# The opening of a hybrid encoder block by halves of the tokens, in another written order, with unread products of a constant on TensorE between its first transposes

## The chip, the core and the metric

The kernel runs on one core of a Trainium2 chip. The time is the device time of one execution in microseconds; lower is better. The engines of a core work side by side from queues of their own: TensorE (PE: matrix products and transposes, with PEld its weight loads), VectorE (DVE), ScalarE (ACT), GpSimd (POOL), and SyncE (SP), which here only issues DMA transfers. Each engine takes its instructions in the order in which they are written, and waits on semaphores for the others.

## The reference, cut to what matters

One layer of an encoder over 512 tokens of width 1024: a SwiGLU feed-forward half step, a token mixer, a second feed-forward half step, each behind an adaptive normalisation. The change lies in the first normalisation and the first columns of the first feed-forward product.

```python
sc = jax.nn.silu(c)
mod = sc @ w_ada[l] + b_ada[l]                 # 1024 -> 9 * 1024
sh1, s1, g1, sh2, s2, g2, sh3, s3, g3 = jnp.split(mod, N_MOD, axis=-1)
h = _modulate(x, sh1, s1)                      # RMSNorm(x) * (1 + s1) + sh1
x = x + 0.5 * g1[:, None, :] * _swiglu(h, ffn1_w_in[l], ffn1_w_out[l])
...                                            # mixer, second feed-forward
```

## The kernel before

Activations lie transposed: a tile has 128 of the 1024 features in its partitions and the tokens along its columns. So the 512 tokens, which come as four blocks of 128 rows in two halves of 512 features (eight tiles `xt`), are first turned on TensorE (`raw`, four transposes and one copy by VectorE for each tile). Products keep nearly full precision: activation and weight are each split into a high and a low part (`hh`/`hl`, `wh`/`wl`), and a product is three passes, high by high, low by high, high by low (lines 304 to 306 elsewhere, 412, 428 and 429 for the first feature tile).

`phase0` is the opening. For each of the eight feature tiles kt it loads 1 MB of `w_ada` (tile `ar`, two transfers) and 384 KB of `ffn1_w_in` (tile `wr`), forms shift and scale of these 128 features (`phase0_cols`, 16 narrow passes on TensorE; `columns`, two products that turn the result into columns, and two small steps on VectorE: `sh`, `s`), normalises the tile (`modulate`: `hm` on VectorE, `hh` on ScalarE, `hl` on VectorE), splits the weights (`wh` cast by ScalarE, `wl` by VectorE), and adds 18 passes of 512 columns to six accumulators `pu`. These are the first six of the 44 columns of tiles of the feed-forward's first product; the others follow in `units`.

Before that stand the sums of squares of x (ScalarE, eight times line 358, each with a read of the accumulator), the mean and its power of -1/2 on GpSimd (`rms_cols`, line 188: `ry`), and for the first feature tile a way of its own: the tokens are scaled by `r` while still untransposed (`xn`), turned (line 394), and modulated (lines 396 to 401). For the other tiles r is spread over the partitions by a product of ones with a diagonal matrix (`dg`, line 476), copied to `rb` (line 414).

The opening is written out in one order, and every instruction of it is made to follow the one before on its engine (`in_order`), so nothing in it is moved by a scheduler. SP issues the transfers in the order of the calls; there are three buffers for `ar` and four each for `wr`, `wh`, `wl`, and five PSUM buffers `pb` beside three `pa`.

Of the kernel before, what the change touches and what calls it, by code (L numbers as in the profile page):

```python
# [19 lines left out]
P = 128  # L20
# [68 lines left out]
class Block:  # L89
# [226 lines left out]
    def setup(self):  # L316
        nc, ins = self.nc, self.ins
        self.vecs = self.slot(s="vecs")[:, :P]
        self.load(self.vecs[72:80, :], ins["c"].rearrange("o (t p) -> (o t) p", p=P))
        self.load(self.vecs[0:72, :], ins["b_ada"].rearrange("o (t p) -> (o t) p", p=P))  # L320
        xd = ins["x"][0]
        self.xtok = [[self.slot(s="xt") for _ in range(2)] for _ in range(NB)]
        for b in range(NB):
            for j in range(2):
                self.load(self.xtok[b][j], xd[b * P:(b + 1) * P, j * NT:(j + 1) * NT])
# [7 lines left out]

    def phase0(self):

        nc = self.nc
# [3 lines left out]
        loads = [self.phase0_load(0), self.phase0_load(1)]  # L340
        pv = self.aux()
        nc.tensor.transpose(pv[:, :80], self.vecs[:80, :], self.ident[:80, :80])
        self.sc = self.const([P, 8], s="sc")
        nc.scalar.activation(self.sc, pv[:, 72:80], AF.Silu)
        self.vT = self.const([P, 72], s="vT")
        nc.vector.tensor_copy(self.vT, pv[:, :72])
        self.sel4 = self.const([P, 1], s="sel4")
        nc.vector.tensor_reduce(out=self.sel4, in_=self.ident[:, 0:P:32], axis=AX.X, op=ALU.add)

        def raw(b, j):  # L350
# [3 lines left out]
            nc.vector.tensor_copy(xall[:, 4 * j:4 * j + 4, b * P:(b + 1) * P], pt.rearrange("p (t c) -> p t c", t=4))  # L354

        tiles = [(b, j) for b in range(NB) for j in range(2)]
        for b, j in tiles:
            nc.scalar.activation(self.slot(s="jk"), self.xtok[b][j], AF.Square, accum_out=ss[:, 2 * b + j:2 * b + j + 1])
        for i in (2, 0, 1, 3):
            raw(*tiles[i])  # L360
        v = self.small(NB, "v")
        nc.vector.tensor_reduce(out=v, in_=ss.rearrange("p (b j) -> p b j", j=2), axis=AX.X, op=ALU.add)
        r = self.rms_cols(v, NB, D)
        for i in (4, 5, 6):
            raw(*tiles[i])
        self.c1, self.c2 = self.const([P, KT], s="sh"), self.const([P, KT], s="s1")
        self.new_h()

        def columns(kt, sg, pg):
            k = slice(kt, kt + 1)  # L370
            for m in range(2):
                nc.tensor.matmul(pg[:, 256 + m:257 + m], sg[:, m * P:m * P + P], self.sel4, start=True, stop=True)
            nc.vector.tensor_tensor(out=self.c1[:, k], in0=pg[:, 256:257], in1=self.vT[:, k], op=ALU.add)
            nc.vector.scalar_tensor_tensor(out=self.c2[:, k], in0=pg[:, 257:258], scalar=1.0, in1=self.vT[:, 8 + kt:9 + kt],
                                           op0=ALU.add, op1=ALU.add)

        def weights(kt):
            raw, hi, lo = loads[kt][1]
            self.split_w(raw[:, :6, :], hi[:, :6, :], lo[:, :6, :])
            return hi, lo  # L380


        xn = self.slot(s="xn")
        for b in range(NB):
            nc.vector.tensor_scalar(out=xn[:, b * P:(b + 1) * P], in0=self.xtok[b][0][:, :P], scalar1=r[:, b:b + 1],
                                    scalar2=None, op0=ALU.mult)
        dg = self.diag(r)
        cols = self.phase0_cols(0, loads[0][0])
        raw0, wh, wl = (x[:, :6, :] for x in loads[0][1])
        w = wh, wl  # L390
        nc.scalar.copy(wh, raw0)
        pt = self.aux()
        for b in range(NB):
            nc.tensor.transpose(pt[:, b * P:(b + 1) * P], xn[:, b * P:(b + 1) * P], self.ident)
        t, m = self.slot(s="hm"), self.slot(s="hm")
        nc.vector.tensor_copy(t, pt)
        columns(0, *cols)
        hh, hl = self.h[0]
        nc.scalar.activation(hh, t, AF.Identity, scale=self.c2[:, 0:1], bias=self.c1[:, 0:1])
        nc.vector.tensor_scalar(out=m, in0=t, scalar1=self.c2[:, 0:1], scalar2=self.c1[:, 0:1], op0=ALU.mult, op1=ALU.add)  # L400
        nc.vector.tensor_tensor(out=hl, in0=m, in1=hh.bitcast(F32), op=ALU.subtract)
        nc.vector.tensor_tensor(out=wl, in0=raw0, in1=wh.bitcast(F32), op=ALU.subtract)
        raw(*tiles[7])
        pu = [self.acc() for _ in range(3)] + [self.aux() for _ in range(3)]
        for kt in range(KT):
            (hi, lo), (xh, xl) = w, self.h[kt]
            more = kt + 1 < KT
            if kt + 2 < KT:
                loads.append(self.phase0_load(kt + 2))
            if kt == 0:  # L410
                for j in range(6):
                    nc.tensor.matmul(pu[j], hi[:, j, :], xh, start=True, stop=False)
# [1490 lines left out]
```

## Time and profile before

| | us |
|---|---|
| median of 3 runs | 1080.29 (1079.97 to 1081.68) |
| profiled execution, own time | 1081.6 |
| its span, first to last instruction | 1079.9 |
| TensorE busy | 1057.4 (98%) |
| VectorE busy | 566.7 (52%) |
| ScalarE busy | 383.9 (36%) |

Times of rows are us from the start of the span. A busy share is an average: TensorE is busy nearly throughout, but in the first 20 us it is not. "Granted clock" is TensorE's clock as a share of 2.4 GHz; 0.5 is 1.2 GHz. The idle time that a row names is that just before the instruction, with what ended it.

### The profile page before, as it was taken

To read this page: it belongs to the slowest core of one execution; us is meant where nothing else is said; L and a number is where in the kernel's file an instruction comes from. 1 tells how busy PE (TensorE), PEld (TensorE's weight loads), DVE (VectorE), ACT (ScalarE), POOL (GpSimd) and SP (SyncE) were. 2 spreads that over 40 slices of the span, in tenths; PEclk is the share of its full clock that TensorE was granted. 3 is DMA by queue.
4 is the path that set the end of the run, shared out by engine and by line. 5 is a ranking of instruction groups with operands and counts; after the bars stand their busy time and mean duration, and the time that the engine had idled before them with its cause. 6 is when DMAs were issued, how large, how long until landed. Compare 5 with 4: busy or idle time off the path is not lost.

```text
span 1079.9 us, 14096 instructions
## 1 busy us (share of the span) xinstructions
PE 1057.4 (98%) x5601; PEld 881.9 (82%) x5601; DVE 566.7 (52%) x1000; ACT 383.9 (36%) x641; POOL 25.8 (2%) x74
## 2 busy tenths in 40 slices
PE   6999999999999999999999989999999999999998
PEld 4788878788887798888788778998888888888887
DVE  4478983433586437559797477573333333322220
ACT  3342222222222226465855553352222222222220
POOL 1000000000000000100000002000000000000000
PEclk8999999999999999999999999999999999999999
DMA  9979973233697335210332121004333333333320
GB/s 273 276 219 317 291 217 107 80 96 93 202 289 260 93 88 162 79 39 20 79 88 55 38 75 41 26 22 135 98 98 97 96 95 95 90 100 108 100 71 30
DMA packets 207760, 130.59 MB, mean 121 GB/s; under 512 B 13633, under 2 KB 191822, under 8 KB 207694
## 3 DMA queue, kind: packets, MB, share of 16 engines
q1 hardware_dynamic: 207694, 129.69, 41.2%
q8 instruction: 44, 0.72, 0.3%
q14 instruction: 22, 0.18, 0.1%
HBM read 127.18 MB, written 2.49 MB: 120 GB/s over the span
## 4 chain that ended last, share of the span: by engine, by line
PE 91%; DVE 5%; ACT 1%; DMA 1%; POOL 1%; issue 1%; SPq 0%; ACTq 0%; POOLq 0%
PE pa L304 26%; PE pa L306 26%; PE pa L305 26%; PE pb L1635 1%; PE pb L1615 1%; DMA ar<-in_w_ada 1%; PE pb L305 1%; PE pb L304 1%; PE pb L306 1%; PE pb L453 1%; PE pb L527 1%; PE pb L1237 1%; POOL ry L188 1%; DVE cv L1181 1%; DVE wl L203 0%
## 5 line engine op out<-in xcount | busy, mean ns | idle before, releaser
L202 ACT CAST wh<-wr 128x1024 fp32r<-128x1024 f32 (+1 forms) x164 | 166.9, 1020 | 482.9 <-PE pa L305 322.7
L304 PE MATMUL pa<-hh,wh 128*128 128x512 f32 (+1 forms) x837 | 324.9, 388 | 0.4 <-DVE cv L1181 0.4
L306 PE MATMUL pa<-hh,wl 128*128 128x512 f32 (+1 forms) x837 | 322.0, 385 | 1.4 <-DVE wl L203 1.4
L305 PE MATMUL pa<-hl,wh 128*128 128x512 f32 (+1 forms) x837 | 321.8, 384 | 1.1 <-DVE hl L490 1.1
L203 DVE TENSOR_TENSOR wl<-wr,wh 128x1024 fp32r<-128x1024 f32 (+1 forms) x164 | 194.3, 1187 | 231.1 <-ACT wh L202 225.4
L304 PEld LDWEIGHTS pa<-hh,wh 128*128 128x128 f32 x837 | 157.4, 188 | 34.3 <-issue 2.9
L306 PEld LDWEIGHTS pa<-hh,wl 128*128 128x128 f32 x837 | 157.4, 188 | 32.5 <-DVE wl L203 2.1
L305 PEld LDWEIGHTS pa<-hl,wh 128*128 128x128 f32 x837 | 157.5, 188 | 30.5 <-DVE hl L490 1.4
L304 PE MATMUL pa<-ah,wh 128*128 128x512 f32 (+1 forms) x396 | 146.3, 370 | 0.0
L306 PE MATMUL pa<-ah,wl 128*128 128x512 f32 (+1 forms) x396 | 144.9, 366 | 0.0
L305 PE MATMUL pa<-al,wh 128*128 128x512 f32 (+1 forms) x396 | 144.8, 366 | 0.0
L304 PEld LDWEIGHTS pa<-ah,wh 128*128 128x128 f32 x396 | 74.7, 189 | 13.5 <-ACT wh L202 1.7
L306 PEld LDWEIGHTS pa<-ah,wl 128*128 128x128 f32 x396 | 74.7, 189 | 12.2
L305 PEld LDWEIGHTS pa<-al,wh 128*128 128x128 f32 x396 | 74.7, 189 | 11.9
L658 DVE TENSOR_TENSOR af<-sg,pa 128x512 f32<-128x512 f32 x40 | 27.5, 686 | 103.0 <-PE pa L306 103.0
L612 DVE SCALAR_TENSOR_TENSOR aa<-ar,sc,aa 128x512 f32<-128x512 f32 x98 | 73.2, 750 | 14.5 <-DMA ar<-in_w_ada 13.4
L720 DVE SCALAR_TENSOR_TENSOR xT<-pa,mod,xT 128x512 f32<-128x512 f32 (+1 forms) x18 | 12.4, 692 | 50.1 <-PE pa L306 49.9
L660 ACT CAST ah<-af 128x512 fp32r<-128x512 f32 x44 | 27.4, 622 | 19.7 <-DVE af L658 19.7
L304 PE MATMUL pa<-mh,wh 128*128 128x256 f32 (+1 forms) x96 | 32.6, 341 | 0.0
L305 PE MATMUL pa<-ml,wh 128*128 128x256 f32 (+1 forms) x96 | 30.9, 322 | 0.3 <-DVE ml L1663 0.3
L661 DVE TENSOR_TENSOR al<-af,ah 128x512 fp32r<-128x512 f32 x44 | 30.2, 686 | 1.5 <-ACT ah L660 1.4
L306 PE MATMUL pa<-mh,wl 128*128 128x256 f32 (+1 forms) x96 | 30.7, 320 | 0.0
(375 smaller groups left out, 1076.9 us busy)
## 6 DMA issues: line engine op xcount, KB each, us to landing
wr<-in_ffn_w_in SPq DMA_DIRECT2D x79, 512.0 KB, 3.9
ar<-in_w_ada SPq DMA_DIRECT2D x48, 512.0 KB, 6.2
wr<-in_ffn_w_out SPq DMA_DIRECT2D x32, 512.0 KB, 4.1
ar<-in_w_ada SPq DMA_DIRECT2D x48, 256.0 KB, 5.1
wr<-in_w_in SPq DMA_DIRECT2D x21, 512.0 KB, 3.8
wr<-in_ffn_w_out SPq DMA_DIRECT2D x16, 384.0 KB, 4.5
wr<-in_w_out SPq DMA_DIRECT2D x8, 512.0 KB
wr<-in_ffn_w_in SPq DMA_DIRECT2D x8, 384.0 KB, 7.3
```

The lines of the kernel that those rows point to most:

```text
L188: nc.gpsimd.tensor_tensor(out=y, in0=v, in1=self.mhalf[:, :n], op=ALU.pow)
L202: self.nc.scalar.copy(hi, raw)
L203: self.nc.vector.tensor_tensor(out=lo, in0=raw, in1=hi.bitcast(F32), op=ALU.subtract)
L304: mm(out, wh, xh, start=start, stop=False)
L305: mm(out, wh, xl, start=False, stop=False)
L306: mm(out, wl, xh, start=False, stop=stop)
L453: nc.tensor.matmul(pg[32 * q:32 * q + 32, :256], self.sc[:, kc:kc + 1].to_broadcast([P, 32]), a[:, kc], start=(e == 0), stop=(e == 1), til ...
L612: nc.vector.scalar_tensor_tensor(out=acc, in0=a, scalar=sc, in1=acc, op0=ALU.mult, op1=ALU.add)
L658: nc.vector.tensor_tensor(out=a, in0=s, in1=pu, op=ALU.mult)
L660: nc.scalar.copy(ah, a)
L661: nc.vector.tensor_tensor(out=al, in0=a, in1=ah.bitcast(F32), op=ALU.subtract)
L720: nc.vector.scalar_tensor_tensor(out=self.xT[t][:, ts], in0=p[:, ts], scalar=gate[:, t:t + 1], in1=self.xT[t][:, ts], op0=ALU.mult, op1=AL ...
```

## The change

The eight token tiles are loaded in two halves (`load_x`): the first four at the head of the queue, ahead of c and b_ada, the other four behind the first `w_ada` tile. Sums of squares, r, `xn`, `dg`, `rb` and the first feature tile's `hh`, `hl` are formed for the first 256 tokens, then for the other 256. The 18 passes of 512 columns of the first feature tile become 18 of 256 columns for each half. Between the first transposes stand 25 products of the constant tile `ones` with itself into a corner of the first accumulator (`busy`), which nobody reads: the first real product there starts the accumulation anew. From the second feature tile on the same passes stand in another order: the first three accumulators' passes are grouped by operand, and the next tile's columns and modulation stand between the groups; `wl` of the next tile comes ahead of its `hl` on VectorE.

The diff, cut to what decides the order:

```diff
-        self.load(self.vecs[72:80, :], ...)
-        self.load(self.vecs[0:72, :], ...)
-        for b in range(NB):
-            for j in range(2):
-                self.load(self.xtok[b][j], ...)
+        self.load_x(0)
+        self.load(self.vecs[72:80, :], ...)
+        self.load(self.vecs[0:72, :], ...)
...
-        loads = [self.phase0_load(0), self.phase0_load(1)]
+        loads = [[self.phase0_ada(0)]]
+        self.load_x(1)
+        loads[0].append(self.phase0_w(0))
+        loads.append([self.phase0_ada(1), self.phase0_w(1)])
...
+        def busy(n):
+            for _ in range(n):
+                mm(pu[0][:, :P], self.ones, self.ones, start=True, stop=True)
+        busy(5)
+        for b, j in ((0, 0), (0, 1), (1, 0)):
+            square(b, j)
+            raw(b, j)
+            busy(3)
+        square(1, 1)
+        r = factors(0)
+        raw(1, 1)
+        pv = self.aux()
+        nc.tensor.transpose(pv[:, :80], self.vecs[:80, :], self.ident[:80, :80])
+        nc.scalar.activation(self.sc, pv[:, 72:80], AF.Silu)
+        v.tensor_copy(self.vT, pv[:, :72])
+        busy(6)
+        xn = scaled(0, r)
+        dg = self.diag(r)
+        pt = turned(xn)
+        spread(0, dg)
+        busy(3)
+        cols = self.phase0_cols(0, loads[0][0], lambda: square(2, 0))
+        raw(2, 0)
+        columns(0, *cols)
+        square(2, 1)
+        first_h(0, pt, lambda: raw(2, 1))
+        w = high(0)
+        square(3, 0)
+        square(3, 1)
+        low(0)
+        raw(3, 0)
+        raw(3, 1, lambda: factors(1))
+        xn = scaled(1, r)
+        dg = self.diag(r)
+        busy(2)
...
+        products(0, 0, first=True)
+        products(0, 1)
+        products(0, 2)
+        pt = turned(xn)
+        first_h(1, pt)
+        cols = self.phase0_cols(1, loads[1][0])
+        spread(1, dg)
+        nw = high(1)
+        products(1, 0)
+        columns(1, *cols)
+        self.h_tile(1, rb, lambda: low(1))
+        products(1, 1)
+        products(1, 2)
+        for kt in range(1, KT):
...
+            for j in range(3):
+                mm(pu[j], hi[:, j, :], xh, ...)
+            if more:
+                cols = self.phase0_cols(kt + 1, loads[kt + 1][0])
+                nw = high(kt + 1)
+            for j in range(3):
+                mm(pu[j], hi[:, j, :], xl, ...)
+            if more:
+                columns(kt + 1, *cols)
+                self.h_tile(kt + 1, rb, lambda: low(kt + 1))
+            for j in range(3):
+                mm(pu[j], lo[:, j, :], xh, ...)
+            for j in range(3, 6):
+                for n, (a, x) in enumerate(((hi, xh), (hi, xl), (lo, xh))):
+                    mm(pu[j], a[:, j, :], x, ...)
```

How three queues stand. First SP at the head of the transfers (`vecs` holds c and b_ada; `wr` at the end is the first feature tile's weight). Before, from the last two token tiles on:

```order
L127 DMA xt_82<-in_x 128x512
L127 DMA xt_83<-in_x 128x512
L127 DMA ar_108<-in_w_ada 128x8x128 x2
L127 DMA wr_109<-in_ffn_w_in 128x2x384
L127 DMA ar_115<-in_w_ada 128x8x128 x2
L127 DMA wr_116<-in_ffn_w_in 128x2x384
```

After, from the fourth token tile on:

```order
L127 DMA xt_77<-in_x 128x512
L127 DMA vecs_73<-in_c 8x128
L127 DMA vecs_73<-in_b_ada 72x128
L127 DMA ar_125<-in_w_ada 128x8x128 x2
L127 DMA xt_78<-in_x 128x512
L127 DMA xt_79<-in_x 128x512
L127 DMA xt_80<-in_x 128x512
L127 DMA xt_81<-in_x 128x512
L127 DMA wr_132<-in_ffn_w_in 128x2x384
L127 DMA ar_136<-in_w_ada 128x8x128 x2
```

The first `w_ada` tile moved ahead of half of x, the first weight tile kept its place behind all of x.

ScalarE around the cast of that weight tile, before:

```order
L358 ACTIVATE jk_144,ss_107<-xt_83 128x512
L456 COPY sg_231<-pb_222 128x256
L391 CAST wh_110<-wr_109 128x768
L399 ACTIVATE hh_196<-hm_239,sh_194,s_195 128x512
L414 COPY rb_275<-pb_276 128x512
```

After:

```order
L534 COPY sg_234<-pb_225 128x256
L352 ACTIVATE jk_248,ss_103<-xt_79 128x512
L389 ACTIVATE hh_109<-pb_216,sh_104,s_105 128x256
L406 CAST wh_133<-wr_132 128x768
L352 ACTIVATE jk_261,ss_103<-xt_80 128x512
L352 ACTIVATE jk_263,ss_103<-xt_81 128x512
L389 ACTIVATE hh_109<-pb_313,sh_104,s_105 128x256
L534 COPY sg_329<-pb_320 128x256
L384 COPY rb_143<-pb_331 128x256
L406 CAST wh_140<-wr_139 128x768
```

The last two squares, which the second half's r needs, moved behind the cast.

TensorE between the first feature tile's products, before:

```order
L412 MATMUL pb_261<-hh_196,wh_110 128x512
L476 MATMUL pb_276<-dg_217,ones_97 128x512
L453 MATMUL pb_279<-ar_115,sc_124 32x256 x8
L428 MATMUL pa_256<-hl_197,wh_110 128x512
L429 MATMUL pa_256<-hh_196,wl_111 128x512
```

After:

```order
L460 MATMUL pb_294<-hh_109,wl_134 128x256
L377 MATMUL pb_313<-ident_88,xn_284 128x128 x2
L529 MATMUL pb_320<-ar_136,sc_106 32x256 x8
L554 MATMUL pb_331<-dg_287,ones_93 128x256
L460 MATMUL pa_144<-hh_109,wh_133 128x256
```

The second half's transposes, the next tile's columns and the second spread stand between all products of the first half and the first of the second.

## Rows read from the trace of the kernel before

**Rows 1.** The page: busy time, share of the span and instructions by engine.
```profile
PE 1057.4 (98%) x5601; PEld 881.9 (82%) x5601; DVE 566.7 (52%) x1000; ACT 383.9 (36%) x641; POOL 25.8 (2%) x74
```
**Rows 2.** Busy time in stretches (stretch, length, each engine, clock, DMA share, GB/s).
```profile
0.00:20.00 20.00, 10.18 (x60) 8.44 (x61) 9.38 (x25) 9.18 (x22) 2.84 (x28) 0.89 0.91 263
60.00:270.00 210.00, 210.00 (x935) 171.31 (x935) 129.32 (x213) 64.76 (x83) 0.00 (x0) 1.00 0.60 180
```
**Rows 3.** TensorE's timeline of the opening (start, duration, what; idle before).
```profile
6.19 4.88 PE L353 MATMUL pb<-ident,xt 128*128 128x128 f32 x28 [2.69 <-DMA xt<-in_x]
14.74 1.09 PE L453 MATMUL pb<-ar,sc 128*32 128x256 f32 x16 [3.67 <-DMA ar<-in_w_ada]
...
18.76 1.65 PE L412 MATMUL pa<-hh,wh 128*128 128x512 f32 x3 [0.28 <-ACT hh L399]
...
21.49 1.57 PE L476 MATMUL pb<-dg,ones 128*128 128x512 f32 x2
...
27.43 1.09 PE L453 MATMUL pb<-ar,sc 128*32 128x256 f32 x16
```
**Rows 4.** TensorE, second and third tile (stretch, length, busy, clock, DMA share, GB/s).
```profile
27.43:33.50 6.07, 6.07 (x40) 1.00 1.08 291
33.50:39.28 5.78, 5.78 (x40) 1.00 1.12 311
```
**Rows 5.** TensorE alone in stretches of 2 us (busy, clock, DMA share, GB/s).
```profile
14.00:16.00 2.00, 1.26 (x17) 0.94 1.12 324
16.00:18.00 2.00, 2.00 (x11) 0.50 1.17 291
...
22.00:24.00 2.00, 2.00 (x18) 0.85 1.11 322
```
**Rows 6.** The first transposes by form, from 6.1 to 8.8, then 9.0 to 11.1.
```profile
L353 PE MATMUL pb<-ident,xt 128*128 128x128 f32 x12 | 2.8, 425 | 2.7 <-DMA xt<-in_x 2.7
L353 PE MATMUL pb<-ident,xt 128*128 128x128 f32 x17 | 2.4, 289 | 0.1
```
**Rows 7.** SP's queue of transfers at the start.
```profile
0.80 0.41 SPq L127 DMA_DIRECT2D vecs<-in_c  x1
...
1.62 3.68 SPq L127 DMA_DIRECT2D xt<-in_x  x8
```
**Rows 8.** The chain in order of time: the first `w_ada` tile's last landing.
```profile
5.84 8.77 DMA ar<-in_w_ada
```
**Rows 9.** ScalarE's timeline: the last square, the copy of sums, the first cast.
```profile
11.07 0.63 ACT L358 ACTIVATE jk<-xt 128x512 f32<-128x512 f32 x1
11.60 0.19 ACT L358 ACTIVATION_READ_ACCUMULATOR jk<-xt 128x1 f32 x1
15.91 0.37 ACT L456 COPY sg<-pb 128x256 f32<-128x256 f32 x1 [4.12 <-PE pb L453]
16.17 0.84 ACT L391 CAST wh<-wr 128x768 fp32r<-128x768 f32 x1
```
**Rows 10.** TensorE in a late stretch of passes of 256 columns.
```profile
1058.00:1068.00 10.00, 10.00 (x82) 1.00 0.08 26
```
**Rows 11.** GpSimd's power, and VectorE's scaling of four token blocks.
```profile
12.27 1.02 POOL L188 TENSOR_TENSOR ry<-ve,mhalf 128x4 f32<-128x4 f32 x1 [10.27 <-DVE ve L580]
...
13.89 0.86 DVE L385 TENSOR_SCALAR xn<-xt,ry 128x128 f32<-128x128 f32 x4
```
**Rows 12.** TensorE's columns in the second tile's stretch, VectorE and ScalarE after them.
```profile
30.22 0.50 PE L372 MATMUL pb<-sel,sg 128*128 128x1 f32 x4
...
31.02 0.75 DVE L496 SCALAR_TENSOR_TENSOR hm<-xT,s,rb 128x512 f32<-128x512 f32 x1
...
31.81 0.72 ACT L498 ACTIVATE hh<-hm,sh 128x512 fp32r<-128x512 f32 x1 [2.09 <-DVE hm L496]
```
**Rows 13.** All engines in two later stretches (columns as in the second group).
```profile
54.00:60.00 6.00, 6.00 (x40) 4.41 (x39) 2.85 (x9) 1.83 (x3) 0.00 (x0) 1.00 0.46 110
...
108.00:114.00 6.00, 6.00 (x28) 4.95 (x28) 6.00 (x16) 1.05 (x1) 0.00 (x0) 1.00 0.98 305
```

More of the change, by code (lines that the diff above doesn't have):

```diff
@@ L332, in setup, with load_x @@
         nc.scalar.activation(self.small(1, "warm"), self.ones[:, 0:1], AF.Silu)
+    def load_x(self, half):
+        for b in (2 * half, 2 * half + 1):
+            for j in range(2):
+                self.load(self.xtok[b][j], self.ins["x"][0][b * P:(b + 1) * P, j * NT:(j + 1) * NT])
     def phase0(self):
-        nc = self.nc
+        nc, mm, v = self.nc, self.nc.tensor.matmul, self.nc.vector
         xall = self.const([P, KT, NT], s="xT")
@@ L361, in phase0 @@
[L361 to L367, printed above, removed]
+            if between:
+                self.r1 = between()
+            v.tensor_copy(xall[:, 4 * j:4 * j + 4, b * P:(b + 1) * P], pt.rearrange("p (t c) -> p t c", t=4))
@@ new lines, in turned, with spread, first_h @@
+        def turned(xn):
+            pt = self.aux()
+            for b in range(2):
+                nc.tensor.transpose(pt[:, b * P:(b + 1) * P], xn[:, b * P:(b + 1) * P], self.ident)
+            return pt
+        rb = self.slot(s="rb")
+        def spread(half, dg):
+            pr = self.spread_diag(dg, 2)
+            nc.scalar.copy(rb[:, half * HALF:half * HALF + HALF], pr[:, :HALF])
+        def first_h(half, pt, between=None):
+            hh, hl = (x[:, half * HALF:half * HALF + HALF] for x in self.h[0])
+            m = self.slot(s="hm")[:, :HALF]
+            nc.scalar.activation(hh, pt[:, :HALF], AF.Identity, scale=self.c2[:, 0:1], bias=self.c1[:, 0:1])
+            v.tensor_scalar(out=m, in0=pt[:, :HALF], scalar1=self.c2[:, 0:1], scalar2=self.c1[:, 0:1], op0=ALU.mult,
+                            op1=ALU.add)
+            if between:
+                between()
+            v.tensor_tensor(out=hl, in0=m, in1=hh.bitcast(F32), op=ALU.subtract)
@@ L369, in columns @@
         def columns(kt, sg, pg):
+            for m in range(2):
+                mm(pg[:, 256 + m:257 + m], sg[:, m * P:m * P + P], self.sel4, start=True, stop=True)
             k = slice(kt, kt + 1)
[L371 to L375, printed above, removed]
@@ new lines, in columns, with high, low @@
+            v.scalar_tensor_tensor(out=self.c2[:, k], in0=pg[:, 257:258], scalar=1.0, in1=self.vT[:, 8 + kt:9 + kt],
+                                   op0=ALU.add, op1=ALU.add)
+        def high(kt):
+            raw, hi, lo = (x[:, :6, :] for x in loads[kt][1])
+            nc.scalar.copy(hi, raw)
+            return hi, lo
+        def low(kt):
+            raw, hi, lo = (x[:, :6, :] for x in loads[kt][1])
+            v.tensor_tensor(out=lo, in0=raw, in1=hi.bitcast(F32), op=ALU.subtract)
+        pu = [self.acc() for _ in range(3)]
```

129 lines of the change are left out of this document (54 added, 75 removed).

## The prediction

> **What bounds the kernel now.** I read the page first: TensorE is busy 1057.4 of 1079.9 us [rows 1]. From 60 to 270 us it is busy without a break [rows 2], so a pass that starts earlier there ends the kernel earlier by as much, unless something else runs out. The first 20 us are different: TensorE is busy 10.18 of them [rows 2]. The timeline says what it waits for: until 6.19 for x, then 3.67 us for the first `w_ada` tile, and the first real product starts at 18.76 [rows 3]. The first tile's products end where line 453 comes for the third time, at 27.43 [rows 3]; from there each further tile takes a stretch of 6.07 and then 5.78 us [rows 4].
>
> Then the clock. Its column reads 0.94 from 14 to 16 us, 0.50 from 16 to 18 and 0.85 from 22 to 24 [rows 5]: solving for the edges, it fell from 2.4 to 1.2 GHz near 15.8 and rose near 22.6. Ahead of the fall TensorE had stood idle 3.67 us and then run 16 narrow passes [rows 3]; ahead of the rise it had run products since 18.76. The column also gives 1.0 for the first microseconds, but the durations contradict it: the transposes until 8.8 take 425 ns each, twelve filling the time from 6.19, those from 9.0 take 289 ns, seventeen in 2.1 us [rows 6]. So the opening starts at 1.2 GHz, is at 2.4 GHz from about 8.9, and loses it again from 15.8 to 22.6, exactly where the first tile's products stand. That is the stretch the change is about.
>
> **The change part by part.** Transfers. x's first tile is issued at 0.80 in place of 1.62 [rows 7], so the stream of large transfers starts 0.82 us earlier; c and b_ada (40 KB) now stand in the middle of it. All of x, the first `w_ada` tile and the first weight tile are the same bytes in sum, so the weight tile lands 0.8 earlier. When it lands now: `w_ada` ends at 14.61 [rows 8], 384 KB at 291 to 324 GB/s [rows 5] are 1.2 to 1.35 us more, so 15.8; an upper bound is 16.17, where the cast runs straight behind a copy on ScalarE [rows 9], the lower one 14.61. After the change I take L = 15.0, with 13.8 to 16.2 as ends; `w_ada` itself, now ahead of half of x, lands some 4 us earlier than before and no longer holds TensorE up.
>
> The products of the constant. 25 products of two passes of 128 columns are 50 passes. A transpose of that width takes 0.22 us at the lower and 0.125 at the upper clock [rows 6]; so 11 us, or 6.2. They stand in TensorE's queue ahead of transposes, but TensorE has 9.8 idle microseconds there [rows 2], and what follows does not hang on TensorE: the first r hangs on ScalarE's squares and GpSimd, the first columns on `w_ada`, the first product on L. Cost nothing; without that cover the last eleven would cost 1.4 to 2.4.
>
> The first half. The first transposes waited for x's third tile until 6.19 [rows 3]; 0.8 earlier and one tile on (256 KB, 0.9) the fourth is there at 6.3, `ry` by the 0.72 and 1.5 below at 8.5, the turned tokens by 9.5. `w_ada` lands at 14.61 less 0.8 less 1 MB at 300 GB/s, 3.5, so 10.3; with TensorE's queue ahead of it the columns are done between 12 and 14, `hh` by 14.8. All that is before the cast's end at L + 0.84 [rows 9]: the first product comes near 16.0 in place of 18.76. 18 passes of 256 columns take 82 per 10 us, so 0.122 each [rows 10], 2.2 us: done at 18.4. Over both halves 36 such passes are 4.4 us.
>
> The second half sets the end. Behind the cast ScalarE has two squares, 0.72 each [rows 9]; so L + 2.2 counting overlapped starts. From the end of the last square to the end of `ry` it is 11.79 to 13.29, 1.5 [rows 9, 11]: L + 3.7. Two scalings of four that take 0.86 [rows 11], with a start 0.1 later: L + 4.3. Two transposes, 0.25. Then TensorE's own order: columns of the second tile, 1.09 [rows 3]; the spread at full clock, a fourth of 1.57 (half the columns, twice the clock) [rows 3], 0.4; six passes, 0.7; the two products of `columns`, 0.5 [rows 12]: L + 7.2. From there it is the chain that the rows of the second tile show: line 372 starts at 30.22 and `hh` ends at 32.53 [rows 12], 2.3 with the 0.5 in it, so 1.8 more: L + 9.0, and the hand-over 0.1. So the second tile's first product starts at T = 24.1. Its weights are then there: TensorE's remaining 12 passes of 0.122 end before, at about 23.8, and the next late one is this `hh`.
>
> What that is worth: before, the second tile's stretch began with line 453 at 27.43 [rows 4]; now the same work (18 passes of 512 and one line 453) begins at 24.1. That is 3.3. Of the second tile's extra 0.29 over the third [rows 4], waiting for a low part, I count all as gone, since `wl` and `hl` are ahead now; bounds 0 and 0.3. **Sum: 3.6 us**, with L's ends 2.4 to 4.8.
>
> From the second tile on, the order is new and the number of passes is not. The first group of a stretch needs only `hh`; the next tile's columns start 0.7 + 1.1 + 0.7 = 2.5 into it, and `hh` ends 2.3 later [rows 12], 4.8 of 5.78. Slack 1.0; cost nothing. Transfers run at about 300 GB/s and a stretch needs 1.44 MB, 4.8 us, also under 5.78.
>
> **Clock and the transposes.** With the constant's products TensorE works almost without pause from 1.3 us on; the longest gap in my timeline is 18.4 to 19.4, where the second half's r is late. Before, gaps of 2.69 and 3.67 us stood [rows 3], and the fall followed the longer. I take the clock as high from some 5 to 8 us until the end.
>
> A rule speaks against that. The rise near 8.9 followed nothing but transposes since 6.19 [rows 6], so here transposes bring the upper clock. The Trainium skill ("TensorE: Matmul & The Clock Gate", section "Part 4: PE-mode transpose") says that full clock does not engage for transposes. By that page the stretch from 12 to 16, which is transposes and narrow columns, would let the clock fall as before and the result would be the first rival's; by the rows it stays, and the sum stands.
>
> **The rivals.** (1) The clock falls again near 15.8, for the same 6.8 us [rows 5]: the work between the second half's r and T takes twice as long: columns 1.1, spread 0.4, transposes 0.25, six passes 0.7, `columns` 0.4, and the first half's 18 passes end 0.6 behind the second half's `xn` instead of ahead. About 3.4 more, T = 27.5; only 0.2 is left: 1080.0. For it: from 12 to 16 TensorE has transposes and narrow columns again, as around the first fall; against: the rise behind transposes [rows 6] and the missing gap.
>
> (2) The gain is eaten later. VectorE is busy 6.00 of 6 us from 108 to 114 at a DMA share of 0.98 [rows 13]; if that work, not TensorE, set the pace there, 3 us earlier would meet it. Then 1079.8. Against: TensorE waits nowhere from 60 to 270 [rows 2], and at 54 to 60 the DMA share is 0.46 [rows 13], so what comes later starts earlier too.
>
> (3) Slower: in the new stretches ScalarE's cast of the next weights stands ahead of the next `hh`, so a late weight tile now holds `hh` and with it the first group. The slack is 1.0 per stretch; at 1.44 MB the transfers must take over 5.8 us, under 250 GB/s, before it costs anything, and under about 215 GB/s (6.7 us per stretch, 0.9 times 7 lost) before it passes the 3.6. Then 1083. Against: 291 to 324 GB/s in every row.
>
> (4) The change doesn't do what it says: the constant's products don't matter, since loading in halves alone closes the gaps. That gives the forecast's time too; only the explanation would differ.
>
> **How the numbers follow.** The profiled execution's own time is 1081.6, 1.7 around its span; the median of the three runs is 1080.29, 1.3 lower. If the 1.3 lies around the span or in the profiling, the median becomes 1080.29 - 3.6 = 1076.7; if it is the opening that went better in those runs, the gain against the median is 2.3, 1078.0. I forecast **1077.3**, own range 1075.5 to 1078.7. Chances: forecast (with rival 4) 0.70, rival (1) 0.12, (2) 0.10, (3) 0.06, an even earlier L 0.02. About 0.2% (2.2 us) is what a measurement of this kernel can tell from no change, so faster means under 1078.1: most of the forecast's case, 0.64; same: its upper end, (1) and (2), 0.29; slower: 0.07. The range 1075.2 to 1079.7 takes in the forecast's case and the better part of (1) and (2).
>
> **What would show it.** In the changed profile: a clock of 1.0 from 8 us on without a second stretch of 0.5 (else rival 1); the cast at about 15.0 (L), the first 256-column product near 16, the second squares ending 2.2 and `ry` 3.7 behind L; the second tile's first 512-column product near 24.1; stretches of 5.8 from there, without TensorE waiting for ScalarE (else rival 3); no new idle time of TensorE from 60 to 270 (else rival 2). The prediction is wrong in its size if the second half's chain is longer than 9.1 from L, and wrong in kind if T moves to 24 and the end does not follow.

## The result, and the profile after

The changed kernel takes 1083.21 us (median of 10, 1082.16 to 1085.46) against 1081.09 (10, 1079.97 to 1082.99) of the kernel before, run beside it: a ratio of 1.0022, interval 1.0012 to 1.0032. It is slower by 0.2%, where 1077.3 was forecast. The profiled execution's own time is 1082.4, its span 1080.7; before they were 1081.6 and 1079.9.

The page's line of busy time by engine (answers [rows 1]):

```profile
PE 1062.6 (98%) x5671; PEld 888.7 (82%) x5671; DVE 566.9 (52%) x1003; ACT 384.6 (36%) x643; POOL 26.2 (2%) x75
```

70 products and 70 weight loads more. 50 of each are the constant's 25 products, in two passes each; 20 of each come from the halves. Then busy time by stretch (answers [rows 2, 4, 5]; columns as in [rows 2]):

```profile
0.00:20.00 20.00, 17.59 (x126) 16.05 (x127) 9.24 (x26) 9.06 (x23) 2.73 (x13) 1.00 0.96 286
...
60.00:270.00 210.00, 210.00 (x936) 171.46 (x935) 128.56 (x211) 63.72 (x83) 0.00 (x0) 1.00 0.59 178
...
25.30:31.22 5.92, 5.92 (x38) 4.33 (x39) 3.25 (x7) 1.83 (x3) 0.00 (x0) 1.00 1.06 285
31.22:37.05 5.83, 5.83 (x40) 4.23 (x38) 2.52 (x5) 1.83 (x3) 0.00 (x0) 1.00 1.09 314
...
14.00:16.00 2.00, 2.00 (x20) 2.00 (x20) 1.36 (x5) 1.61 (x5) 0.00 (x0) 1.00 1.17 291
16.00:18.00 2.00, 2.00 (x16) 1.81 (x15) 2.00 (x4) 1.33 (x5) 0.00 (x0) 1.00 1.10 323
...
22.00:24.00 2.00, 2.00 (x19) 1.97 (x18) 0.48 (x3) 1.11 (x2) 1.14 (x32) 1.00 1.13 323
```

TensorE now works 17.59 of the first 20 us, the clock does not fall in the opening any more, and from 60 to 270 there is still no break. So the part that the change is about did go as meant, though less far. TensorE's timeline of the opening (answers [rows 3]):

```profile
3.53 1.09 PE L357 MATMUL pb<-ident,xt 128*128 128x128 f32 x4
...
12.24 1.09 PE L529 MATMUL pb<-ar,sc 128*32 128x256 f32 x16
...
16.15 0.62 PE L460 MATMUL pa<-hh,wh 128*128 128x256 f32 x3
...
18.27 0.52 PE L460 MATMUL pb<-hh,wl 128*128 128x256 f32 x3
19.87 0.43 PE L377 MATMUL pb<-ident,xn 128*128 128x128 f32 x2 [1.08 <-DVE xn L370]
20.24 1.09 PE L529 MATMUL pb<-ar,sc 128*32 128x256 f32 x16
21.54 0.70 PE L554 MATMUL pb<-dg,ones 128*128 128x256 f32 x2 [0.22 <-DVE hm L390]
...
25.30 0.96 PE L482 MATMUL pa<-hh,wh 128*128 128x512 f32 x3 [0.47 <-ACT hh L504]
```

The second tile's first product (T of the prediction) stands at 25.30. From the first transposes at 3.53 to the end of the first half's products near 18.8 the timeline shows no pause of TensorE; the rows of the constant's products add up to 8.9 us. ScalarE, VectorE and GpSimd in the same stretch (answers [rows 9, 11]):

```profile
14.81 0.57 ACT L389 ACTIVATE hh<-pb,sh,s 128x256 fp32r<-128x256 f32 x1 [0.39 <-DVE s L401]
15.28 0.82 ACT L406 CAST wh<-wr 128x768 fp32r<-128x768 f32 x1
...
16.62 0.62 ACT L352 ACTIVATE jk<-xt 128x512 f32<-128x512 f32 x1
16.80 0.95 DVE L411 TENSOR_TENSOR wl<-wr,wh 128x768 fp32r<-128x768 f32 x1
...
17.67 0.68 DVE L360 COPY xT<-pb 128x512 f32<-128x512 f32 x1
18.27 0.15 DVE L364 TENSOR_REDUCE v<-ss 128x2 f32<-128x4 f32 x1
...
18.70 0.70 POOL L188 TENSOR_TENSOR ry<-ve,mhalf 128x2 f32<-128x2 f32 x1 [8.85 <-DVE ve L658]
19.44 0.48 DVE L370 TENSOR_SCALAR xn<-xt,ry 128x128 f32<-128x128 f32 x2 [0.23 <-POOL ry L188]
```

Behind the opening TensorE's instructions stand in the same order in both kernels, so each record of the one trace can be set against its twin in the other (times here are those of the kernel before). The changed kernel is 2.00 us ahead at 66 us, 1.96 at 510 and 1.97 at 543. Then it loses: 0.43 ahead at 552, 1.00 behind at 572, 0.8 behind from 590 to the end. **The whole loss, 2.8 us, lies between 543 and 590 us, in the token mixer, where the change touched no line.**

There the mixer sends a tile through DRAM and back to rearrange it, in pieces of 64 bytes, twice: first `a_d`, read into `ba`, then `t_d`, read into `t`. VectorE and everything behind it wait for each. SP's issue of the reading and VectorE's first instruction on the data, kernel before:

```profile
544.00 1.35 SPq L1273 DMA_DIRECT2D ba<-a_d  x2
...
547.82 0.16 DVE L969 TENSOR_TENSOR bw<-ba,bt 128x1 f32<-128x1 f32 x1 [0.46 <-DMA ba<-a_d]
...
566.01 0.37 SPq L1293 DMA_DIRECT2D t<-t_d  x1
569.69 0.69 DVE L969 TENSOR_TENSOR t<-t,mk 128x512 f32<-128x512 f32 x1 [1.89 <-DMA t<-t_d]
```

And the changed kernel (its line numbers are 78 higher):

```profile
542.05 1.34 SPq L1351 DMA_DIRECT2D ba<-a_d  x2
547.39 0.16 DVE L1047 TENSOR_TENSOR bw<-ba,bt 128x1 f32<-128x1 f32 x1 [1.97 <-DMA ba<-a_d]
...
565.58 0.37 SPq L1371 DMA_DIRECT2D t<-t_d  x1
570.69 0.69 DVE L1047 TENSOR_TENSOR t<-t,mk 128x512 f32<-128x512 f32 x1 [3.33 <-DMA t<-t_d]
```

The first reading takes 5.34 in place of 3.82, the second 5.11 in place of 3.68: 2.95 us in sum. The view of DMA queues (packets, MB, share of 16 engines' time), from the first issue to the data, shows one thing more in the changed kernel:

```profile
q1 hardware_dynamic: 2496, 0.56, 51.4%
q8 instruction: 1, 0.02, 1.3%
```

The same view of the kernel before, 544 to 548:

```profile
q1 hardware_dynamic: 2092, 0.14, 41.3%
```

The queue named "instruction" moves packets of 16 KB. The page counts 44 of them, 0.72 MB, in both kernels. TensorE has 11342 products and weight loads, so there is one packet for about every 256 of them, and single packets near the mixer take 0.9 to 1.5 us. Before, they came at 536.9, 555.6 and 582.7, clear of both readings. Now they come at 544.9 (1.10 us) and 568.2 (1.39 us), each inside one. The Trainium skill ("Runtime: NRT & Kernel Launch", section "Instruction fetch mechanics") says that an engine's instructions are fetched in blocks of 16 KiB, 256 instructions, over DMA, and that this is mostly hidden. Size and count agree with the trace; whether it is hidden here is what the experiments ask.

### The profile page after: what moved, and what is told of

Same layout as the page of the kernel before. It is cut to its first block, busy times and chain, and to the rows that moved or that the text cites. A ratio compares the mean times of both kernels' runs of the same rounds, so it can differ in the third digit from the quotient of the medians.

```text
span 1080.7 us, 14250 instructions
## 1 busy us (share of the span) xinstructions
PE 1062.6 (98%) x5671; PEld 888.7 (82%) x5671; DVE 566.9 (52%) x1003; ACT 384.6 (36%) x643; POOL 26.2 (2%) x75
## 4 chain that ended last, share of the span: by engine, by line
PE 44%; DVE 4%; ACT 2%; DMA 1%; POOL 1%; issue 0%; SPq 0%; DVEq 0%; ACTq 0%; POOLq 0%
PE pa L304 12%; PE pa L306 12%; PE pa L305 12%; PE pb L1713 1%; PE pb L605 1%; POOL ry L188 1%; DVE cv L1259 1%; PE pb L1693 1%; DMA t<-t_d 0%; ACT bd L1345 0%; DMA ba<-a_d 0%; PE pb L1396 0%; DVE wl L203 0%; DVE bw L1047 0%; PE pb L1402 0%
## 5 line engine op out<-in xcount | busy, mean ns | idle before, releaser
L202 ACT CAST wh<-wr 128x1024 fp32r<-128x1024 f32 (+1 forms) x157 | 161.1, 1029 | 488.2 <-PE pa L305 332.9
L304 PE MATMUL pa<-hh,wh 128*128 128x512 f32 (+1 forms) x816 | 315.4, 387 | 0.4 <-DVE cv L1259 0.4
L306 PE MATMUL pa<-hh,wl 128*128 128x512 f32 (+1 forms) x816 | 313.5, 384 | 1.4 <-DVE wl L203 1.4
L305 PE MATMUL pa<-hl,wh 128*128 128x512 f32 (+1 forms) x816 | 313.6, 384 | 1.1 <-DVE hl L568 1.1
L203 DVE TENSOR_TENSOR wl<-wr,wh 128x1024 fp32r<-128x1024 f32 (+1 forms) x157 | 187.5, 1196 | 221.8 <-ACT wh L202 215.4
L304 PEld LDWEIGHTS pa<-hh,wh 128*128 128x128 f32 x816 | 153.5, 188 | 31.5 <-ACT wh L202 0.8
L306 PEld LDWEIGHTS pa<-hh,wl 128*128 128x128 f32 x816 | 153.4, 188 | 31.3 <-DVE wl L203 1.7
L305 PEld LDWEIGHTS pa<-hl,wh 128*128 128x128 f32 x816 | 153.5, 188 | 29.9 <-DVE hl L568 1.3
L690 DVE SCALAR_TENSOR_TENSOR aa<-ar,sc,aa 128x512 f32<-128x512 f32 x98 | 73.0, 748 | 11.1 <-DMA ar<-in_w_ada 9.6
L738 ACT CAST ah<-af 128x512 fp32r<-128x512 f32 x44 | 27.4, 622 | 14.7 <-DVE af L736 14.7
```

The lines of the kernel that those rows point to most:

```text
L202: self.nc.scalar.copy(hi, raw)
L203: self.nc.vector.tensor_tensor(out=lo, in0=raw, in1=hi.bitcast(F32), op=ALU.subtract)
L304: mm(out, wh, xh, start=start, stop=False)
L305: mm(out, wh, xl, start=False, stop=False)
L306: mm(out, wl, xh, start=False, stop=stop)
L690: nc.vector.scalar_tensor_tensor(out=acc, in0=a, scalar=sc, in1=acc, op0=ALU.mult, op1=ALU.add)
```

## The experiments

The kernel before was run again beside each group of these: 1081.15 (25 executions), 1080.97 (34) and 1081.14 (15). First theory: the 140 more TensorE instructions move the instruction packets onto the mixer's two readings, and this costs 2.8 us; the opening's gain is real. Rivals: the loss belongs to the new opening or to the mixer's earlier start; or products at the head cost something by themselves.

**Padding the kernel before.** 36 unread products of 32x32 of the constant at its head, 144 TensorE instructions:

```diff
+        pu = [self.acc() for _ in range(3)]
+        pw = pu[0]
+        def pads(n):
+            for _ in range(n):
+                nc.tensor.matmul(pw[:32, :32], self.ones[:32, :32], self.ones[:32, :32], start=True, stop=True)
+        pads(36)
```

> The kernel before with 36 unread products of a 32x32 corner of ones at the head of TensorE's queue, ahead of the first transposes, where TensorE was idle (144 instructions more, as many as the change adds). Theory A (the 16 KB instruction packets, one for about every 256 instructions of TensorE, now fall on the mixer's two round trips through DRAM): the opening stays (second tile's stretch begins near 27.4), the packets move to about 545 and 568 us, VectorE's two waits there grow by 1 to 1.5 us each, and the time rises by 2 to 3.5 us, to 1083 to 1084.5. Theory B (the loss belongs to what the changed opening leaves behind, such as buffers or the order of transfers): the time stays within 1 us of before, 1080 to 1082.

1083.8 us, ratio 1.0029 (1.0018 to 1.0039). The records are 0.32 behind those of the unpadded kernel at 543, 2.15 at 552 and 3.73 at 572: the same loss at the same place, without the change.

```profile
549.97 0.16 DVE L977 TENSOR_TENSOR bw<-ba,bt 128x1 f32<-128x1 f32 x1 [2.27 <-DMA ba<-a_d]
...
573.42 0.69 DVE L977 TENSOR_TENSOR t<-t,mk 128x512 f32<-128x512 f32 x1 [3.48 <-DMA t<-t_d]
```

**Padding the changed kernel** by another 112, so that the packets are some 250 instructions on:

```diff
-        busy(6)
+        busy(2)
+        pads(16)
...
-        pt = turned(xn)
+        pt = turned(xn, 16)
```

The 16 in the last line are products of 32x32 ahead of the second half's transposes.

> The changed kernel with 112 more TensorE instructions: 16 unread products of a 32x32 corner in place of 4 of the 6 large ones behind the transpose of c and b_ada, and 16 in the pause ahead of the second half's transposes. With the change's own 140 this is close to one whole packet of instructions. Theory A: the packets stand where they stood before (near 535 and 554 us, 1 to 2 us earlier with the opening), the two mixer waits are as short as before, the opening's 2 us stay to the end: 1078.5 to 1079.8, about 2 us under before. Theory B: the time stays with the changed kernel's, 1082.5 to 1084.

1079.97 us, ratio 0.9989 (0.9979 to 0.9999): 3.2 under the changed kernel with more work in it, and 0.2 over the range expected. The mixer is as fast as before (table below). Its opening is better too, T at 24.57, 2.71 us ahead. But from 510 to 530 it falls back by 1.60. TensorE's windows there (busy, clock, DMA share, GB/s):

```profile
514.00:516.00 2.00, 0.57 (x3) 1.00 0.00 0
516.00:518.00 2.00, 2.00 (x13) 0.86 0.63 160
518.00:520.00 2.00, 2.00 (x11) 0.50 0.39 110
```

The clock is at 1.2 GHz from 517.4 to 520.8, behind a wait of TensorE of 1.4 us for a low weight part. The kernel before has the same wait (1.43 us, until 518.31) and kept its clock.

**Fewer pads in the kernel before**, 16 in place of 36, and **fewer constants in the changed kernel**, 9 in place of 25 (groups of 2, 1, 1, 1, 2, 1, 1; 76 TensorE instructions over the kernel before):

> The kernel before with 16 unread 32x32 products of the constant at the head (64 more TensorE instructions, in place of 144 of the padded kernel that came out 0.29% slower). First theory (instruction packets of 16 KB that meet the mixer's two round trips through DRAM): the packets, one per some 256 TensorE instructions, move by a quarter of their spacing only, to about 526 and 541 us and then 560 us or so, outside 545 to 547.5; if the next one stays clear of 567 to 570 too, the time is that of the kernel before: 1080.3 to 1081.8, ratio 0.999 to 1.001. Rival (products at the head cost something by themselves, through the opening or the clock): 1082 or more, and the aligned records already apart at 60 us.

> The changed kernel with 9 products of the constant in place of 25 (groups of 2, 1, 1, 1, 2, 1 and 1). It has 78 TensorE instructions more than the kernel before, in place of 140, so the instruction packets move by a third of their spacing and not by half. First theory: the packets stand clear of the two round trips of the mixer, the loss of 2.7 us at 545 to 571 us is not there, and the time is that of the changed kernel less 2.7, plus 0 to 1.7 for a clock that rises later or falls: 1080.3 to 1082.2. Rival (the loss belongs to the new opening, whatever the packets do): 1083 or more, with the mixer as slow as in the changed kernel.

1081.11 (0.9999, 0.9988 to 1.001) and 1080.21 (0.9988, 0.9977 to 0.9998): the first as the first theory has it, the second 0.1 better. The packets of the version with 16 pads stand at 530.2, 551.7 and 581.7, not at 526, 541 and 560 as expected, but clear of both readings all the same. In the version with 9 constants the packets come at 549.0 and 575.1, behind the data of either reading:

```profile
546.14 0.16 DVE L1047 TENSOR_TENSOR bw<-ba,bt 128x1 f32<-128x1 f32 x1 [0.48 <-DMA ba<-a_d]
...
568.09 0.69 DVE L1047 TENSOR_TENSOR t<-t,mk 128x512 f32<-128x512 f32 x1 [2.00 <-DMA t<-t_d]
```

All kernels of the study (TensorE instructions over those of the kernel before; instruction packets near the mixer; from the issue of each reading to VectorE's first use):

| kernel | more | packets at | first reading | second reading |
|---|---|---|---|---|
| before | 0 | 536.9, 555.6 | 3.82 | 3.68 |
| **changed** | 140 | 544.9, 568.2 | **5.34** | **5.11** |
| **changed, second profile** | 140 | 545.7, 568.7 | **5.03** | **5.16** |
| **before, 36 pads** | 144 | 547.4, 570.9 | **5.64** | **5.26** |
| **changed, small constants** | 140 | 546.6, 569.6 | **5.37** | **4.92** |
| before, 16 pads | 64 | 551.7, 581.7 | 3.71 | 3.63 |
| changed, 9 constants | 76 | 549.0, 575.1 | 3.84 | 3.79 |
| changed, both mended | 76 | 547.1, 573.2 | 3.71 | 3.74 |
| changed, padded | 252 | 535.2, 554.6 | 3.84 | 3.76 |
| changed, second half first | 252 | 535.1, 554.2 | 3.60 | 3.58 |
| before, clock | 256 | 535.0, 554.2 | 3.74 | 3.65 |
| before, clock, clear | 256 | 541.0, 561.4 | 3.74 | 3.77 |

In the four profiles of three programs with a packet in each reading both readings are long, in the old order of the opening as in the new; in the eight programs without they are as in the kernel before. The rivals fall. The packet of the both-mended version at 547.1 is no exception, its first reading was over at 544.0.

**Packet by packet.** A reading is 2048 packets of 64 bytes and 32 of 4 bytes. In the changed kernel's second reading 2041 of the 64-byte packets and 31 of the 4-byte ones have begun by 568.5. Then none begins until the instruction packet (568.17 to 569.57) ends, and the last eight follow. The view of DMA queues from 568.50 to 569.54, then from 569.54 to 569.80:

```profile
DMA packets 0, 0.00 MB, mean 0 GB/s; under 512 B 0, under 2 KB 0, under 8 KB 0
```
```profile
q1 hardware_dynamic: 8, 0.00, 5.0%
```

It is so in all eight slow readings: exactly one of the 32 packets of 4 bytes, in seven of them with 7 to 102 of 64 bytes, comes as or after the instruction packet ends, 0.9 to 1.25 us behind the others. In the other versions, and in the two further profiles of the kernel before, the last packet of 4 bytes comes 0.3 us at most behind the one before it.

**The changed kernel profiled again**, unchanged:

> The changed kernel, unchanged: a second profiled execution. First theory (instruction packets at 545 and 568 lie in the mixer's two round trips in every execution): the packets within 1 us of 544.9 and 568.2, and the time from the last product ahead of the mixer to the first behind it as in the first profile; 1082.2 to 1083.6, with a fall of 3.4 us near 517 in an execution at 0.998. Rival (the slow round trips were a chance of one profile): the mixer some 2.7 us shorter, 1079.5 to 1081.

1082.96; packets within 0.8 us of the first profile's, the same loss (1.21 ahead at 543, 1.50 behind at 572).

**Constants of 32x32 in place of 128x128** (same number of instructions):

> The changed kernel with its 25 products of the constant cut to a 32x32 corner: as many instructions at the same places, but a quarter or less of their time on TensorE, so the code packets stay where they are in the changed kernel. If the large products hold the clock: it is lower for longer (up to 7 us more at 1.2 GHz before 25 us), the second tile's first product comes at 27 in place of 25.3, and the time is 1.5 to 2.5 us over the changed kernel's, 1085. If they only stand in the way: the first columns come up to 0.5 us earlier, the second tile's first product at 24.8 to 25.3, and the time is 0 to 0.5 us under the changed kernel's, 1082.5 to 1083.2.

1084.17 us, ratio 1.0038 (1.0025 to 1.005). The clock is at its lower level until 14.9, not 7.06, and T is at 27.00, 1.7 behind the changed kernel's first profile and 0.9 behind its second (26.08). Counted from the first transpose it is 22.88, against 21.77 and 21.87, so 1.0 to 1.1; the medians differ by 1.0 and the ratios by 0.0016, 1.7 us, where 1.5 to 2.5 was expected. So the constants do matter, and the fourth rival is wrong.

**The clock without the halves.** The kernel before with the constant's products alone, 15 large ones in the pause ahead of the first columns, first with 49 pads at the head, then with 20 there and 29 further on:

> The kernel before with 15 unread products of ones (128x128) in the pause between the transposes and the first columns, and 49 of a 32x32 corner at the head: 256 TensorE instructions more, one whole packet, so the code packets stand as before. No halves, no new order. If the pause lowered the clock: no fall at 15.8, the second tile's stretch begins near 24.7 in place of 27.4, and the time is 2 to 2.8 us under before, 1078.3 to 1079.1: as much as the whole change gained in its opening. If the clock's fall is not what the pause did, or the fall cost nothing: 27.4 and 1081.

> The kernel before (whole token tiles, old order) with the constant's products alone, 256 more TensorE instructions, so that the instruction packets fall where they fell before: 20 small products at the head, 24 behind the transposes of the vectors, 15 large and 5 small ones in the pause ahead of the first columns. First theory (the constant's products are what gains, the halves add little): no fall of the clock between 15.8 and 22.6, the first tile's stretch of line 453 at 24.9 to 25.3 in place of 27.43, kept to the end; 1079.0 to 1079.8, as the padded version of the changed kernel (1079.97). Rival (the halves and the new order carry the gain): the stretch stays past 26 or the time over 1080.5.

1081.9 (1.0009, 0.9999 to 1.0018) and 1085.68 (1.0041, 1.0028 to 1.0055). In both the clock held through the opening, and the line that stood at 27.43 [rows 3] stands at 25.95 and 26.16. Against an execution with 6.8 us at the lower clock, the clock alone is thus worth some 1.3 to 1.5 us here; the pads at the head delay the first transposes, so this is likely a lower bound. Neither version tests the total as it was meant to. The first lost nothing further (1.49 ahead to the end) in a profile without a fall of the clock, but its five executions at 1.0 take 1080.6 in the mean, where the kernel before takes 1079.5 at 0.999 or 1.0: over all executions the pads cost more than the clock gave. The second met a new wait at 48 us, on VectorE first, then on TensorE:

```profile
53.91 0.17 DVE L1124 COPY ex<-vb 128x4 f32<-128x4 f32 x1 [5.89 <-DMA vb<-in_gdn_a_log]
53.99 0.74 DVE L502 SCALAR_TENSOR_TENSOR hl<-hm,sh,hh 128x512 fp32r<-128x512 f32 x1
...
54.79 0.50 PE L305 MATMUL pa<-hl,wh 128*128 128x512 f32 x1 [3.67 <-DVE hl L502]
```

A 2 KB load of the mixer, issued at 47.82, landed after 6.1 us; a copy that waits for it stands ahead of `hl` on VectorE. The load was not slow: the view of DMA issues gives 6.1 us for it in the changed kernel too. What differs is the copy's place in VectorE's queue. With 49 pads `hl` comes first, and the copy only behind the next `wl`, `sh` and `s`:

```profile
48.60 0.75 DVE L500 SCALAR_TENSOR_TENSOR hl<-hm,sh,hh 128x512 fp32r<-128x512 f32 x1 [0.79 <-ACT hh L508]
...
53.31 0.17 DVE L1122 COPY ex<-vb 128x4 f32<-128x4 f32 x1 [0.51 <-DMA vb<-in_gdn_a_log]
```

In the other versions the copy waits 0 to 3.1 us and TensorE not at all. Behind the wait of 3.67 us the clock fell from 55.3 to 58.8, so wait and clock make up the 5.6 us between the records at 43 and at 60 us. Why the order of the two differs between these builds was not settled.

**The kernel before profiled twice more**, to see where its clock falls:

> The kernel before, unchanged: a second profiled execution, to see where its clock falls. In 31 of 59 executions of it the mean clock was 0.998 (about 1081.05), in 14 of them 0.999 or 1.0 (about 1079.5); the profiled one on which the prediction rests had 0.997, with a fall from 15.8 to 22.6. First theory (the 0.998 of the changed versions is the fall behind TensorE's pause near 516, and the kernel before has the same pause): a fall of 3.4 us either near 15 or near 517, the rest of the time at 1.0, 1080.5 to 1081.5. Rival (the opening alone makes the clock fall in the kernel before): the fall near 15 again, 3.4 or 6.8 us long, and none near 517.

> The kernel before once more, unchanged, for the same question. First theory: over the three profiled executions the fall stands at more than one place (near 15 or near 517). Rival: near 15 in all three.

1081.89 and 1083.13. The rival was right: the fall is in the opening in all three profiles, from 15.8 to 22.6, 16.2 to 23.1 and 14.2 to 24.4, and none is near 517. But these three have a mean clock of 0.997, 0.997 and 0.995; no profile of the kernel before caught an execution at 0.998, the value in question. The version with 16 pads did, and its fall, 3.4 us long, is in the opening too (14.7 to 18.1). In the changed versions none is in the opening, but three of them (padded, 9 constants, second half first) have one of 3.4 us near 517, as has the version "clock, clear" of the kernel before (at 523, behind the same pause); the changed kernel itself, in two profiles, and the both-mended version have none. So part of what the opening gains in clock is lost again there in some executions. What decides that fall, where the pause is in all versions, stays open.

**The second half's chain.** The padded version with the last two squares ahead of the cast, the factors (`v`) ahead of VectorE's copies and low part, and the first tile's low-part products behind the second half's columns:

> The padded version of the changed kernel (1079.97) with the second half's chain put ahead: its last two squares ahead of the cast on ScalarE, its factors ahead of the copies and the low part on VectorE, the first tile's low-part products behind the second half's columns on TensorE. First theory (the second half's r was late because the cast stood behind hh and the factors behind VectorE's copies): the second half's r near 17.5 in place of 18.7, the second tile's first 512-column product at 23.1 to 23.8 in place of 24.57, kept to the end: 1078.6 to 1079.5. Rival (the cast and the first product, now later, hold TensorE up by as much, or the opening's time is lost again later): 24.4 or later, 1079.8 to 1081.

1079.8 (0.9992, 0.9979 to 1.0004): the rival. `ry` started at 16.45, even earlier than expected, but T came only at 24.58. The cast and with it the first product came 0.9 later than in the padded version (16.31 for 15.42), and from there to T TensorE has no idle time; the 16 pads (32 passes, 1.19 us) are part of that work.

**Both mended**: that order, with the 9 constants and without pads:

> The changed kernel with 9 products of the constant in place of 25 and the second half's chain put ahead (last two squares ahead of the cast, factors ahead of VectorE's copies and low part, the first tile's low-part products behind the second half's columns), without the small products that stood ahead of the second half's transposes. 78 TensorE instructions more than the kernel before, as the version with 9 products that gave 1080.21. First theory: packets stand clear of the mixer; ry near 16.6, the second tile's first 512-column product at 22.9 to 23.7 in place of 24.06; 1079.4 to 1080.2 (0 to 1.0 under that version). Rival (weights or the first half's products hold that product where it is): 24.0 or later and 1080.2 to 1081.

```profile
15.70 0.15 DVE L364 TENSOR_REDUCE v<-ss 128x2 f32<-128x4 f32 x1
...
16.13 0.81 POOL L188 TENSOR_TENSOR ry<-ve,mhalf 128x2 f32<-128x2 f32 x1 [6.96 <-DVE ve L670]
...
23.63 0.88 PE L494 MATMUL pa<-hh,wh 128*128 128x512 f32 x3
```

1078.14 us against 1081.14, ratio 0.9982 (0.9972 to 0.9992): it beats both kernels, and is 1.3 better than the range expected; six of its eleven executions are at a clock of 1.0. T is at 23.63, and the records are 3.75 ahead at 66 us, 3.72 at 543 and 3.74 at 1060: with the packets clear of the readings, all that the opening gains reaches the end.

## Why the prediction was wrong

**Right.** The reading of the opening: TensorE's pauses and the clock's fall were what could be won, the constants bring the clock up early (7.06 and 7.97 in the two profiles of the changed kernel, with no fall after; 14.9 with small constants, which cost 1.0 to 1.7), the first rival did not occur, and from 14 to 16 us, where TensorE has mostly transposes, the clock stayed at 1.00. The weight tile came at 14.76 for a forecast L of 15.0, the first product at 16.15 for 16.0. "A pass that starts earlier there ends the kernel earlier by as much" held over the stretch that I had read, and in the both-mended version to the end. The second rival named a later loss, but the wrong one, VectorE and bandwidth near 108 to 114 us: the records are 2.00 ahead at 66 us and 2.02 at 250. The third did not occur in the changed kernel. Its price is off: by its own slack it would pass 3.6 at 6.3 us per stretch, some 229 GB/s, and not at 215.

**The step that failed: "Cost nothing", for the 25 products.** I looked for what hides them in TensorE's queue alone, found 9.8 idle microseconds, and took zero. That was wrong twice.

First in the opening, where it mis-sized T: forecast at 24.1, it came at 25.30. The text had named the sign itself, a chain longer than 9.1 from L: with the weight tile at 14.76 the chain took 10.54. The cast, which was to start at L, waited behind `hh` until 15.28, 0.52. The last square was read 2.05 later (2.2 forecast). `ry` was done 2.07 behind that, where 1.5 stood, because `v` waited behind two of VectorE's copies, `hl` and the low part until 18.27. From `ry` to T it took 5.90, where 5.4 stood.

The version with 9 products shows which of these the products caused:

```profile
3.72 1.09 PE L357 MATMUL pb<-ident,xt 128*128 128x128 f32 x4 [1.30 <-DMA xt<-in_x]
...
10.99 1.09 PE L529 MATMUL pb<-ar,sc 128*32 128x256 f32 x16
...
14.67 0.83 ACT L406 CAST wh<-wr 128x768 fp32r<-128x768 f32 x1 [0.54 <-DMA wr<-in_ffn_w_in]
...
17.02 0.15 DVE L364 TENSOR_REDUCE v<-ss 128x2 f32<-128x4 f32 x1
...
24.06 0.96 PE L482 MATMUL pa<-hh,wh 128*128 128x512 f32 x3 [0.48 <-ACT hh L504]
```

There the weight tile came at 14.65, and the same four steps take 0.02, 2.08, 1.41 and 5.90. The waits of the cast and of `v` are gone; the 0.5 between `ry` and T stays, an error of its own (0.2 of it TensorE's wait for VectorE's `hm`). That T stands at 24.06, where the prediction had it, is therefore partly luck: the weight tile was 0.35 earlier than L. Of the 16 products taken out 15 stand ahead of the first columns, in a queue that has no pause left there; the columns stand ahead of twelve transposes and of `hh`, and from there the delay goes on in ScalarE's queue (the cast, then the last squares) and VectorE's (`v`). The prediction looked for the cover on the wrong engine: ScalarE and VectorE wait for what TensorE does next. Its price for lost cover, 1.4 to 2.4, counts the last eleven products as eleven passes; they are 22, by its own rows 2.8 to 4.8, and took 3.0.

These are single profiles, and T moves between executions of one program: the second profile of the changed kernel has it at 26.08, its first tile of x having come 0.7 later. Counted from the first transpose, T is 21.77 and 21.87 in the changed kernel, 20.34 with 9 products and 19.90 with both mended. So the 16 products are worth 1.4 to 1.5 us, and the order of the second half's chain, which that last version changes on three engines at once, 0.4 more.

A smaller term is the new order of the stretches, 5.92 and 5.83 for 6.07 and 5.78 [rows 4]. T is 2.13 earlier than the 27.43 before, but the records only 2.00 at 66 us: of the 0.29 that was counted nothing was won, and 0.13 was lost. So 1.2 at T and 0.4 in the stretches are what the opening lacks.

Second, they are instructions. With the 20 pairs that the halves bring they shift all that is fetched behind them by 140 of some 256, and that put two packets onto the mixer's readings, for 2.8 us. The page had the queue ("q8 instruction: 44, 0.72", 0.3% of the time) and I passed over it for its share.

In sum against the profiled execution: 3.6 forecast, 1.6 missing in the opening, 2.8 lost in the mixer; 0.8 slower is what it shows.

**Which part is shown, and which argued.** Shown: four profiles with a packet in each reading lose 2.5 to 3.2 us there, ten without (three of them of the kernel before) lose 0.1 at most, and the number of TensorE instructions ahead moves a kernel from one side to the other, in the old order as in the new. Shown too: the last part of each slow reading starts moving when the instruction packet ends. One packet of 0.9 to 1.5 us thus makes a whole reading late through the few small ones that come last. Argued: that these few stand behind it on one of the 16 DMA engines. The Trainium skill ("DMA: Bandwidth & Descriptors", section "Queues, rings and completion order") says that a DMA engine changes between queues only from packet to packet, which would have this effect. One late packet of 4 bytes in 32 fits that, but the trace does not tell the engine of a packet.

**The reference of the sum.** It was made against an execution in which the clock was low for 6.8 us. By mean granted clock the executions of the kernel before take 1079.5 (18 at 0.999 or 1.0) and 1081.0 (36 at 0.998); the both-mended version 1077.9 (6) and 1079.6 (4), the one with 9 constants 1078.7 (4) and 1080.4 (7). At the same clock the halves are thus worth 1.4 to 1.6 us at best and 0.7 to 0.9 as the change has them without the packets; as far as these means tell, the rest of the forecast's 3.6 is the clock, and that some executions of the kernel before kept anyway.

## What to carry to other kernels

An instruction that an idle engine can take for nothing is still fetched: where a change adds a hundred of them ahead of a step that waits for many small transfers, look where the instruction packets fell there before, and time a version with a few dozen more or fewer before judging the change. Align the records of both traces over the whole span and look where the difference changes; it may be half a millisecond behind the edit. When costing a chain over several engines, write down the queue of each of them, the copies included. Profile one program twice before giving a cause to a few tenths of a microsecond: here the same opening differed by 0.8.

## What the runs showed of the hardware

- One instruction packet of 16 KB for about every 256 TensorE instructions, near the mixer 0.9 to 1.5 us long. Inside a reading of 64-byte pieces it added 1.2 to 1.8 us to the 3.6 to 3.9 that the reading takes: a few of the pieces begin only as it ends.
- In the changed kernel the clock rose at 7.06 and 7.97 us (two profiles), behind products of a constant and transposes from 1.2 us on; with 32x32 products only at 14.9. In the kernel before it rose at 8.93, 12.82 and 10.79, behind nothing but transposes, most of them since 6.19, 7.01 and 7.15.
- The column of granted clock reads 1.00 from 4 to 6 us in the changed kernel, where a transpose takes 424 ns as at the lower level [rows 6]: ahead of its first event the column says nothing.
- The same pause of 1.4 us, near 516 us in most versions, is followed by 3.4 us at 1.2 GHz in four of the fourteen profiles and by none in ten; the fall costs 1.6 us.
